# A hybrid decoder trunk on one core: modulation sums by transposes and in float32r, a 128-row gate product, and state products next to their value sums

## The chip, the cores and the metric

The kernel runs on one core of a Trainium2 chip. The metric is the device time of one execution in microseconds (us), as the median of several runs. A profile of one further execution shows each instruction of the engines: TensorE (PE, its weight loads as PEld), VectorE (DVE), ScalarE (ACT), GpSimd (POOL), and SyncE (SP), which issues most of the DMAs.

## What is computed

Two layers, each on x of 1024 tokens by 1024 columns, all in float32. In each, a conditioned norm, one wide projection to three groups of heads, and an output projection:

```python
c_act = silu(c)                                  # one row of 1024
mod = c_act @ w_mod + b_mod                      # 3072 columns
shift, scale, gate = split(mod, 3)
h = rms_norm(x, pre_gain) * (1 + scale) + shift
proj = h @ w_in                                  # 3088 columns
# A: sliding-window softmax attention; B: retention; C: gated linear attention
gate_logits = ga @ gla_gate_w + gla_gate_b       # rank 16, 128 columns
log_a = log_sigmoid(gate_logits) / 16
# C, per chunk: out = intra(scores, v) + (q * exp(b)) @ state
#               state = exp(b_last) * state + (k * exp(b_last - b)).T @ v
y = concat(a_out, r_out, g_out) @ w_out
x = x + gate * rms_norm(y, post_gain)
```

The change touches three pieces: the row `mod`, the `gate_logits`, and the state of C.

## The kernel before

Tokens are worked in 8 tiles of 128, in pairs p = 0 to 3. The large projections (`accum`, L521) are products of 128x128 weights with up to 512 columns, three passes over 8 blocks each: both factors are kept as a rounded float32r half and a float32r remainder in the tile `arena`, and the product of the two remainders is left out. Their sums go to PSUM tiles `mm` (3 banks); everything else goes to `aux` (5 banks). All matmuls are recorded by the helper `mult` (L171) and all transposes by `transp` (L186), so the profile names them by tiles. A product of plain float32 operands appears in the profile as two records for one instruction of the program, a float32r product and a transpose as one.

Working tiles come from shared pools: `t1` (256 columns, 7 buffers) and `t2` (512 columns, 14 buffers), both shown as `t`; `st` is a stage for weights, `sm` holds small columns.

The order on TensorE is fixed by a planner written in the kernel. It keeps a clock `clk`, to which `mult` and `transp` add an estimate per instruction. Jobs are generators: `yield lat("gc3", l)` means "come back when the clock has gone on by the time listed under that key", and `yield (t, flag)` waits for a flag as well. Between the products of a projection `pump` (L216) runs the jobs that are due. So another estimate, or a step on the other side of a `yield`, moves what follows by a few products. The orders of the other engines are laid out by the framework's scheduler from the same program.

- `mod_third(l, j)` (L356) makes one third of `mod` for a layer, in two halves `hh` of 512 columns. DVE accumulates 8 weight blocks, scaled by `c_act`, into `acc` of 128x512 (L384). The sum over the 128 partitions remains. For shift and scale (j < 2) it is wanted as a column: four products with `acc` as weights and one column of ones, then `mod_cols` (L288) adds the bias. For the gate (j = 2) it is wanted in every partition: ones (128x128) times `acc`, fp32, out 128x512, then a multiplication into `modg` (L398). Layer 0's shift and scale are made elsewhere (`mod_first`); `mod_third` runs with j = 2 in both layers, and with j = 1 and 0 for layer 1 while layer 0 is at work. Hence four column sums of four products each, and four gate sums.
- `gla_log` (L1068) multiplies `gwt` (17 of 32 rows used: 16 weights and the bias) with `gat`, the transposed low-rank columns and a row of ones; 32 rows by 512 columns, fp32, twice per layer. `new_ga` (L800) takes `gat` as a slice of a 128-partition buffer and fills it with ones on POOL.
- `gla_core` (L1136) is one pair of tiles of C. After `gc2`: a transpose of the keys to `kbn`, block products for the two tiles (out `bx`, `bd`), masking into `sc`; then the state products into `pst` (L1182: for each tile and head, 32 rows by 64 columns of output, fp32); then the delays `gc3` and `gc4`; then the value sums `within` (L1008: out 64x128, fp32, `aux<-sc,t`), for the first tile the product with the old state (`aux<-t,stG`), the update of `stC` from `pst` (L1202) and its spread to `stG` (L1203), both on DVE, a delay `gc6`, and the second tile's product with `stG`. The second update is the last reader of the decay factors `gs`, whose two buffers are cleared on POOL (L1117). The last pair has state products for its first tile only.

Of the kernel before, what the change touches and what calls it, by code (L numbers as in the profile page):

```python
# [10 lines left out]
F32 = mybir.dt.float32  # L11
# [6 lines left out]
P = 128  # L18
# [71 lines left out]
def trunk(ctx: ExitStack, tc: tile.TileContext, ins, cst, out):  # L90
# [79 lines left out]
    def mult(dst, lhsT, rhs, start, stop, cost=None):  # L170
        T.matmul(dst, lhsT, rhs, start=start, stop=stop)  # L171
        if cost is not None:
            clk[0] += cost
            return
        n = 1
        for d in rhs.shape[1:]:
            n *= d
        c = n / 2400.0
        if rhs.dtype == F32R:
            c = max(c, 0.107 if lhsT.shape[-1] > 64 else 0.055)  # L180
        else:
            c = max(4 * c, 0.21 if n > 2 else 0.03)
        clk[0] += c
# [5 lines left out]
    def lat(key, l):  # L189

        return L[key + "@1"] if l and key + "@1" in L else L[key]
# [96 lines left out]
    def mod_cols(l, j, hh, pm, rc):  # L288
        res = modc[(l, j)]
        ks = slice(4 * hh, 4 * hh + 4)  # L290
        if j == 0:
            V.tensor_tensor(res[:, ks], pm[:, 0:4], rc[:, ks], ALU.add)
        else:
            col = small(4)
            V.tensor_tensor(col, pm[:, 0:4], rc[:, ks], ALU.add)
            V.scalar_tensor_tensor(res[:, ks], col, 1.0, rc[:, 8 + 4 * hh:12 + 4 * hh], ALU.add, ALU.mult)
# [59 lines left out]
    def mod_third(l, j):  # L356
        wv = w_mod[l].rearrange("(p k) n -> p k n", k=KT)
        if j < 2:
            mod_tile(l, j)
            rows = mod_rows(l, j)  # L360
            yield lat("mod1", l)
            rc = mod_rows_t(rows)
        else:
            res = cp.tile([P, D], F32, name=nm("modg"), tag="modg")
            modg[l] = res
        for hh in range(2):
            c0 = j * D + 512 * hh
            acc = gp.tile([P, 512], F32, tag="acc", name=nm("acc"), bufs=1)
            if j == 2:
                G.memset(acc, 0.0)  # L370
                nc.sync.dma_start(acc[0:1, :], b_mod[l:l + 1, c0:c0 + 512])
            def fetch(k):
                w_ = stage()
                dma("lwm", w_, wv[:, k, c0:c0 + 512])
                return w_

            coming = fetch(0)
            for k in range(KT):
                wt, coming = coming, fetch(k + 1) if k + 1 < KT else None
                yield lat("mod7", l)  # L380
                if k == 0 and j < 2:
                    V.tensor_scalar(acc, wt, c_act[:, k:k + 1], None, ALU.mult)
                else:
                    V.scalar_tensor_tensor(acc, wt, c_act[:, k:k + 1], acc, ALU.mult, ALU.add)  # L384
                yield lat("mod2", l)
            yield lat("mod3", l)
            pm = aux()
            if j < 2:
                for b in range(4):
                    mult(pm[:, b:b + 1], acc[:, b * P:(b + 1) * P], ones[:, 0:1], True, True)  # L390
                mod_cols(l, j, hh, pm, rc)
                if j == 0:
                    flag(("modh", l, hh), lat("mod4", l))
            else:
                mult(pm, ones, acc, True, True)
                gain = stage()
                nc.sync.dma_start(gain, post_g[l:l + 1, 512 * hh:512 * hh + 512].to_broadcast((P, 512)))
                V.tensor_tensor(res[:, 512 * hh:512 * hh + 512], pm, gain, ALU.mult)  # L398
            yield lat("mod5", l)
        flag(("mod", l, j), lat("mod6", l))  # L400
# [397 lines left out]
    gat = []  # L798

    def new_ga():  # L800
        gat.append(gp.tile([P, NT * P], F32, tag="kT1", name=nm("gaT"), bufs=1)[0:32, 0:512])
        G.memset(gat[-1], 1.0)
    stR = cp.tile([P, 2, P], F32, name="stR")
    stG = cp.tile([P, 4, 64], F32, name="stG")
# [25 lines left out]
    for l in range(DEPTH):  # L830
        V.tensor_copy(sink8[:, l].rearrange("p (m r) -> p m r", r=2),
                      sinkn[:, 8 * l:8 * l + 8].rearrange("p (r m) -> p m r", r=2))
    gwt = cp.tile([32, 2, P], F32, name="gwt")
    V.memset(gwt, 0.0)
    for l in range(DEPTH):
        nc.sync.dma_start(gwt[0:16, l, :], gw_in[l])
# [299 lines left out]
    def gla_core(l, p, qk, vs):  # L1136
# [31 lines left out]
        for c in range(2):  # L1168
            if c:
                yield lat("gc7", l)  # L1170
            bx, bd = h4(aux()), h4(aux())
            for s in range(1, 4):
                q = slice(32 * s, 32 * s + 32)
                mult(bx[:, :, q], kxz[:, s - 1, c], qx[:, :, c, q], True, True)
            for s in range(4):
                i = slice(8 * s, 8 * s + 8)
                mult(blocks(bd)[:, :, :, i], kds[s][:, P * c:P * c + P], blocks(qd[:, :, c])[:, :, :, i], True, True)
            A.activation(scz[c][:, :, 32:P], bx[:, :, 32:P], AF.Copy)
            V.copy_predicated(scz[c], mask2.unsqueeze(1).to_broadcast((P, 4, P)), bd)
        pst = aux()  # L1180
        for c in range(2):
            if 2 * p + c < NT - 1:  # L1182
                for h in range(4):
                    mult(pst[32 * h:32 * h + 32, 64 * c:64 * c + 64], kbn[:, c * P + 32 * h:c * P + 32 * h + 32],
                         vs[c][:, 64 * h:64 * h + 64], True, True, 0.03)
        yield lat("gc3", l)
        yield lat("gc4", l)
        po = aux()
        for c in range(2):
            within(po, c, vs[c], scz[c])  # L1190
# [449 lines left out]
```

## Time and profile before

| | us |
|---|---|
| median of 3 runs | 957.99 (956.76 to 958.2) |
| the profiled execution | 954.65 |
| its span, first to last instruction | 952.9 |
| mean granted TensorE clock | 0.997 |
| TensorE busy | 932.7 |
| VectorE busy | 637.4 |
| ScalarE busy | 474.1 |
| GpSimd busy | 222.6 |

Busy times count an engine that executes an instruction; TensorE's records overlap, since products are pipelined, and their union is taken. A row of the timeline has start, length, engine, line, operation, tiles (out<-in), shape and count of merged instructions, and in brackets the idle time of the engine before it with what ended it. A row of a group has the busy time, the mean in ns, and the idle time before.

### The profile page before, as it was taken

The page shows a single profiled execution, that of the slowest core. Times are in us where ns is not written, and L with a number is a line of the kernel's source. Part 1 is how long each engine was busy: PE and PEld are TensorE (multiplying, and loading weights), DVE is VectorE, ACT ScalarE, POOL GpSimd, SP SyncE. Part 2 cuts the span into 40 slices and gives each one's busy share as a digit, 9 for nine tenths or more (in the row PEclk, how much of TensorE's full clock was granted, in tenths as well). Part 3 has the DMA queues.
Part 4 walks back from the last instruction along what each step waited for, and adds up shares of the span by engine and source line. Part 5 has one row for each costly group of instructions (what it writes and reads, how often), then busy time and mean ns, then how long its engine had stood idle before and what let it go on. Part 6 is the DMA issues. An engine that isn't in the chain of part 4 may idle for free.

```text
span 952.9 us, 15951 instructions
## 1 busy us (share of the span) xinstructions
PE 932.7 (98%) x5645; PEld 770.1 (81%) x5645; DVE 637.4 (67%) x1372; ACT 474.1 (50%) x1157; POOL 222.6 (23%) x288
## 2 busy tenths in 40 slices
PE   5999999999999999999999999999999999999997
PEld 1799887888888787778889888888888887787886
DVE  6886857757786988654685584694677787862332
ACT  3786233554756666622455532443667576661111
POOL 3222000423231324510131110033133033540000
PEclk9999999999999999999999999999999999999999
DMA  9943523613362345787455261362133222555951
GB/s 320 323 135 122 161 84 122 196 49 115 107 200 80 100 133 189 226 253 256 171 169 175 92 187 32 101 187 67 56 101 111 94 82 81 166 177 177 308 200 66
DMA packets 124651, 142.26 MB, mean 149 GB/s; under 512 B 11566, under 2 KB 95384, under 8 KB 124572
## 3 DMA queue, kind: packets, MB, share of 16 engines
q1 hardware_dynamic: 114396, 127.43, 42.1%
q10 hardware_dynamic: 10176, 13.82, 4.2%
q8 instruction: 44, 0.72, 0.3%
q14 instruction: 35, 0.29, 0.1%
HBM read 104.51 MB, written 36.70 MB: 148 GB/s over the span
## 4 chain that ended last, share of the span: by engine, by line
PE 85%; DVE 3%; issue 2%; ACT 2%; POOL 0%; DMA 0%; DVEq 0%; SPq 0%; POOLq 0%; ACTq 0%
PE mm L171 67%; PE aux L171 14%; PE aux L186 4%; ACT smx L971 0%; DMA t<-tabS 0%; ACT L1026 0%; DVE t L856 0%; ACT L1025 0%; DVE t L1029 0%; DVE t L1027 0%; DVE t L157 0%; ACT mx L1160 0%; DVE smx L966 0%; DVE arena L508 0%; DVE arena L149 0%
## 5 line engine op out<-in xcount | busy, mean ns | idle before, releaser
L171 PE MATMUL mm<-arena,arena 128*128 128x512 f32 (+2 forms) x1512 | 309.6, 358 | 0.0
L171 PE MATMUL mm<-arena 128*128 128x512 f32 (+2 forms) x1392 | 285.8, 359 | 0.0
L171 PEld LDWEIGHTS mm<-arena,arena 128*128 128x128 f32 x1512 | 246.5, 189 | 40.1 <-issue 2.1
L171 PEld LDWEIGHTS mm<-arena 128*128 128x128 f32 x1392 | 228.9, 190 | 37.2 <-issue 1.2
L171 PE MATMUL mm<-arena,mx 128*128 128x512 f32 (+1 forms) x696 | 157.3, 384 | 0.0
L171 PEld LDWEIGHTS mm<-arena,mx 128*128 128x128 f32 x696 | 126.5, 188 | 26.1 <-issue 1.5
L508 POOL TENSOR_TENSOR arena<-st,arena 128x512 fp32r<-128x512 f32 x57 | 85.9, 1512 | 158.0 <-ACT arena L147 100.3
L147 ACT ACTIVATE t<-aux 128x512 f32<-128x512 f32 x64 | 37.1, 591 | 82.6 <-PE aux L186 39.6
L508 DVE TENSOR_TENSOR arena<-st,arena 128x512 fp32r<-128x512 f32 x63 | 63.0, 1014 | 6.9 <-ACT arena L147 3.5
L147 ACT ACTIVATE arena<-st 128x512 fp32r<-128x512 f32 x82 | 48.4, 623 | 31.1 <-PE mm L171 15.0
L1285 ACT ACTIVATE t<-mm 128x512 f32<-128x512 f32 x30 | 17.9, 598 | 91.0 <-PE mm L171 46.3
L971 ACT ACTIVATE smx<-smx,sm 128x129 f32<-128x129 f32 x128 | 50.1, 394 | 18.1 <-DVE sm L968 17.9
L975 POOL TENSOR_TENSOR smx<-smx,sm 128x512 f32<-128x512 f32 x32 | 35.2, 1099 | 82.5 <-DVE sm L974 78.7
L384 DVE SCALAR_TENSOR_TENSOR acc<-st,c_act,acc 128x512 f32<-128x512 f32 x60 | 45.6, 760 | 13.1 <-DMA st<-in_w_mod_dram 12.1
L562 POOL TENSOR_TENSOR sm<-sm,few 128x1 f32<-128x1 f32 x26 | 14.8, 570 | 150.3 <-DVE sm L561 147.6
L1286 DVE TENSOR_TENSOR t<-mm,modg 128x512 f32<-128x512 f32 x30 | 20.7, 689 | 42.4 <-ACT t L1285 42.4
L1330 DVE SCALAR_TENSOR_TENSOR t<-t,sm,t 128x512 f32<-128x512 f32 x32 | 25.5, 827 | 30.8 <-DMA t<-xs 15.7
L186 PE MATMUL aux<-c_ident,t 128*128 128x128 f32 x224 | 33.7, 274 | 4.1 <-DVE t L634 2.3
L186 PEld LDWEIGHTS aux<-c_ident,t 128*128 128x128 f32 x224 | 26.6, 140 | 10.5 <-DVE t L634 2.7
L966 DVE COPY_PREDICATED smx<-c_curmask,aux 128x256 f32<-128x256 int32 x64 | 25.5, 447 | 12.8 <-ACT smx L147 11.4
L370 POOL MEMSET acc<- 128x512 f32 x4 | 2.1, 529 | 130.2 <-PE aux L171 119.1
L851 DVE TENSOR_TENSOR t<-mm,sincos 128x128 f32<-128x128 f32 (+2 forms) x36 | 16.2, 450 | 23.7 <-ACT t L147 12.5
(223 smaller groups left out, 1340.5 us busy)
## 6 DMA issues: line engine op xcount, KB each, us to landing
st<-in_w_in_dram SPq DMA_DIRECT2D x96, 256.0 KB, 3.9
st<-in_w_mod_dram SPq DMA_DIRECT2D x64, 256.0 KB, 3.0
mixS<-t SPq DMA_DIRECT2D x64, 256.0 KB, 2.5
mx<-mixS SPq DMA_DIRECT2D x28, 512.0 KB, 5.2
st<-in_w_out_dram SPq DMA_DIRECT2D x32, 256.0 KB, 3.2
wm<-in_w_mod_dram SPq DMA_DIRECT2D x12, 512.0 KB, 4.7
t<-in_x_dram SPq DMA_DIRECT2D x24, 256.0 KB, 4.9
t<-tabS SPq DMA_DIRECT2D x16, 256.0 KB
```

The lines of the kernel that those rows point to most:

```text
L147: A.activation(dst, src, AF.Copy)
L171: T.matmul(dst, lhsT, rhs, start=start, stop=stop)
L186: T.transpose(dst, src, idn)
L384: V.scalar_tensor_tensor(acc, wt, c_act[:, k:k + 1], acc, ALU.mult, ALU.add)
L508: i = (G if first == 0 and kc in LOG else V if first == 0 else eng(f"wlo{kc}")).tensor_tensor(wt[:, 1, 2 * kc:2 * kc + 2, 0:256], st, f(hi ...
L851: V.tensor_tensor(a4, s4, cs.unsqueeze(1).unsqueeze(1).to_broadcast((P, nh, 2, 32)), ALU.mult)
L966: V.copy_predicated(sv, curmask.unsqueeze(1).to_broadcast((P, 2, P)), pv[:, :, n // P - 1, :])
L971: A.activation(sm[:, h, :], sm[:, h, :], AF.Exp, bias=mx[:, h:h + 1], accum_out=sums[:, h:h + 1])
L975: eng("pn").tensor_tensor(sm[:, :, 0:128], sm[:, :, 0:128], rs.unsqueeze(2).to_broadcast((P, 4, P)), ALU.mult)
L1285: A.activation(yg, pm, AF.Square, accum_out=ss[:, nh:nh + 1])
L1286: V.tensor_tensor(yg, pm, modg[l][:, 512 * nh:512 * nh + 512], ALU.mult)
L1330: V.scalar_tensor_tensor(xt[j], yg[j], r, xt[j], ALU.mult, ALU.add)
```

## The change

1. Column sums (j < 2): `acc` is transposed in four blocks of 128 columns into one PSUM bank, and DVE adds each block along its columns (a reduction of 128x512 to 128x4).
2. Gate sums (j = 2): ScalarE copies the ones and a rounded `acc` (`hi`) to float32r, DVE makes the remainder `lo`, and two float32r products replace the fp32 product. The three new tiles come from `t1` and `t2`.
3. `gwt` and `gat` get 128 rows instead of 32; rows from 17 on of `gwt` are zero.
4. In `gla_core` the two delays come ahead of the state products, so that these stand directly ahead of `within`, and their PSUM bank is taken there.

```diff
@@ mod_third
+            if j == 2:
+                one, hi, lo = t1(F32R), t2(F32R), t2(F32R)
+                A.activation(one[:, 0:P], ones, AF.Copy)
+                A.activation(hi, acc, AF.Copy)
+                V.tensor_tensor(lo, acc, f(hi), ALU.subtract)
             yield lat("mod3", l)
             pm = aux()
             if j < 2:
                 for b in range(4):
-                    mult(pm[:, b:b + 1], acc[:, b * P:(b + 1) * P], ones[:, 0:1], True, True)
-                mod_cols(l, j, hh, pm, rc)
+                    transp(pm[:, b * P:(b + 1) * P], acc[:, b * P:(b + 1) * P], ident)
+                sums = small(4)
+                V.tensor_reduce(sums, pm.rearrange("p (b n) -> p b n", b=4), AX.X, ALU.add)
+                mod_cols(l, j, hh, sums, rc)
                 if j == 0:
                     flag(("modh", l, hh), lat("mod4", l))
             else:
-                mult(pm, ones, acc, True, True)
+                mult(pm, one[:, 0:P], hi, True, False)
+                mult(pm, one[:, 0:P], lo, False, True)
@@ new_ga
-        gat.append(gp.tile([P, NT * P], F32, tag="kT1", name=nm("gaT"), bufs=1)[0:32, 0:512])
+        gat.append(gp.tile([P, NT * P], F32, tag="kT1", name=nm("gaT"), bufs=1)[:, 0:512])
@@ trunk
-    gwt = cp.tile([32, 2, P], F32, name="gwt")
+    gwt = cp.tile([P, 2, P], F32, name="gwt")
@@ gla_core
+        yield lat("gc3", l)
+        yield lat("gc4", l)
         pst = aux()
         for c in range(2):
             if 2 * p + c < NT - 1:
                 for h in range(4):
                     mult(pst[32 * h:32 * h + 32, 64 * c:64 * c + 64], kbn[:, c * P + 32 * h:c * P + 32 * h + 32],
                          vs[c][:, 64 * h:64 * h + 64], True, True, 0.03)
-        yield lat("gc3", l)
-        yield lat("gc4", l)
         po = aux()
```

What this does to the orders is shown at three places. First TensorE in layer 1, first pair, before (each row is an instruction of the program with its count; `mm_7201` is a projection, `aux_7231` the block products, `aux_7241` the state products, `aux_7258` the value sums):

```order
L171 MATMUL aux_7231<-mx_6900,t_1247_7129 128x16x8
L171 MATMUL aux_7241<-t_1228_7041,t_1263_7213 32x64 x4
L171 MATMUL aux_7241<-t_1239_7092,t_1263_7213 32x64 x4
L171 MATMUL mm_7201<-arena_357 128x512 x8
L171 MATMUL aux_7258<-sc_6905,t_1228_7041 64x128 x4
L171 MATMUL aux_7258<-sc_6906,t_1239_7092 64x128 x4
```

And now, with the same parts as `aux_7267`, `aux_7285` and `aux_7294`:

```order
L171 MATMUL aux_7267<-mx_6918,t_1263_7164 128x16x8
L171 MATMUL mm_7237<-arena_357 128x512 x8
L171 MATMUL aux_7285<-t_1244_7076,t_1279_7249 32x64 x4
L171 MATMUL aux_7285<-t_1255_7127,t_1279_7249 32x64 x4
L171 MATMUL aux_7294<-sc_6923,t_1244_7076 64x128 x4
L171 MATMUL aux_7294<-sc_6924,t_1255_7127 64x128 x4
```

The state products went behind the eight projection products and touch the value sums; so they do in all eight pairs. Second, VectorE in layer 0, second pair, before: the masking of the scores (`sc`), then the first state update, and only later its spread:

```order
L1179 COPY_PREDICATED sc_2057<-c_mask_418,aux_2637 128x4x128
L1202 SCALAR_TENSOR_TENSOR stC<-stC,gs_2319,aux_2647 128x64
L1145 TENSOR_TENSOR t_469_2773<-t_394_2362,t_429_2534 128x512
L1032 TENSOR_TENSOR t_436_2562<-t_433_2558,t_435_2561 128x512
L868 TENSOR_TENSOR kT_2168<-aux_2658,kT_2167 128x128
```

And now, at the place of the update (rows L859 to L865 are a rotation of keys):

```order
L876 TENSOR_TENSOR kT_2181<-aux_2707,kT_2180 128x128
L864 TENSOR_TENSOR t_460_2692<-t_461_2693,t_462_2694 128x2x32
L865 TENSOR_TENSOR t_460_2692<-t_461_2693,t_462_2694 128x2x32
L1210 SCALAR_TENSOR_TENSOR stC<-stC,gs_2333,aux_2716 128x64
L1211 TENSOR_TENSOR stG<-stC,c_hmask 128x256
```

The update stands some fifteen rows further back in the queue, directly ahead of its spread. Third, VectorE where the attention scores begin, now: mask copies into `smx`, the new reduction of a column sum (`sm_3710`), the first step of the next accumulator, and the softmax maximum (`sm_3717`):

```order
L974 COPY_PREDICATED smx_3669<-c_curmask,aux_3674 128x2x128
L947 COPY smx_4011<-sink_434 128x4
L947 COPY smx_4029<-sink_434 128x4
L397 TENSOR_REDUCE sm_3710<-aux_3705 128x4
L382 TENSOR_SCALAR acc_3817<-st_3818,c_act 128x512
L295 TENSOR_TENSOR sm_3712<-sm_3710,sm_2391 128x4
L976 TENSOR_REDUCE sm_3717<-smx_3652 128x4
```

Before, the maximum followed its two mask copies at once:

```order
L966 COPY_PREDICATED smx_3636<-c_curmask,aux_3639 128x2x128
L966 COPY_PREDICATED smx_3636<-c_curmask,aux_3640 128x2x128
L968 TENSOR_REDUCE sm_3691<-smx_3636 128x4
L966 COPY_PREDICATED smx_3653<-c_curmask,aux_3657 128x2x128
L939 COPY smx_3994<-sink_434 128x4
```

The column sum came later there, behind the rotations of the queries.

## The prediction

> **What bounds the kernel now.** I read the page's busy times first, then the waits of TensorE, then the chain that ended last, and only then single places of TensorE's timeline. The page:
>
> ```profile
> PE 932.7 (98%) x5645; PEld 770.1 (81%) x5645; DVE 637.4 (67%) x1372; ACT 474.1 (50%) x1157; POOL 222.6 (23%) x288
> PEclk9999999999999999999999999999999999999999
> PE 85%; DVE 3%; issue 2%; ACT 2%; POOL 0%; DMA 0%; DVEq 0%; SPq 0%; POOLq 0%; ACTq 0%
> ```
>
> TensorE is busy in 98% of the span at full clock, and 85% of the chain is its own work. A busy TensorE could still be one that waits inside its queue, so the waits come next (engine and line, what it waited for, us in total, times, longest):
>
> ```profile
> PE aux L186 <- DVE posr L425: 6.1, 1, 6.1
> PE aux L186 <- DVE t L634: 2.3, 1, 2.3
> PE aux L186 <- DVE smx L966: 1.7, 3, 0.9
> ```
>
> These are the three longest. The rows of 6.1 and 2.3 us belong to the start; within the two layers nothing is above 1.7 us, in three pieces. So no other engine sets the pace, and a microsecond of TensorE's issue time removed is a microsecond of the span, unless the new order makes it wait. The unit for this issue time is a projection product, which I take from the longest unbroken piece of the chain:
>
> ```profile
> 871.27 70.05 PE mm L171 x308
> ```
>
> 70.05 / 308 = 0.2274 us each. The durations in the groups are of no use for a sum, because products overlap; I count from start to start and take off 0.2274 us per projection product in between.
>
> **Column sums of the modulation (four times, all in layer 0, for layer 1).** Before: four products of one column, eight records in fp32. After: four transposes.
>
> ```profile
> 462.06 0.60 PE L186 MATMUL aux<-c_ident,t 128*128 128x128 f32 x4
> 462.42 3.00 PE L171 MATMUL mm<-arena,mx 128*128 128x512 f32 x12
> 465.26 0.94 PE L171 MATMUL aux<-c_ones,acc 128*128 128x1 f32 x8
> 466.06 1.19 PE L171 MATMUL mm<-arena,mx 128*128 128x512 f32 x4
> 467.09 1.47 PE L186 MATMUL aux<-c_ident,t 128*128 128x128 f32 x12
> ```
>
> The sums: 467.09 - 465.26 = 1.83, less 4 x 0.2274 = 0.91, gives 0.92 us. Four transposes: 465.26 - 462.06 = 3.20, less 12 x 0.2274 = 2.73, gives 0.47 us. Saved: 0.45 us, four times 1.8 us. The replacement is seen in this very stage, so I give this term no wide bounds.
>
> A rule speaks against this term. The Trainium skill, page "TensorE: Matmul & The Clock Gate", section "Part 4: PE-mode transpose", gives about 275 ns for a transpose in a kernel and says that the full clock does not engage for it; section "Back-to-back issue gap" gives some 60 cycles for a product of up to 64 columns. An estimate by these two: 4 x 0.275 = 1.1 us against 8 x 0.025 = 0.2 us, so 0.9 us lost each time, 3.6 us in all, and a sum of 1.0 us instead of 6.4, 957.0 us. The trace has the transposes at a pitch that fits neither: four cost 0.47 us with the clock at 9 throughout, and the eight records cost 0.92, each with a weight load of its own (the page counts 5645 loads to 5645 products). I take the rows.
>
> **Gate sums (four times, two per layer).** Before: ones times the accumulated 128x512 in fp32. After: the accumulator in a rounded half and a remainder, two products in float32r. The same pair, with the same shape, stands in every head norm (out aux, in t and bones).
>
> ```profile
> 150.20 1.02 PE L171 MATMUL aux<-acc,c_ones 128*128 128x512 f32 x2
> 150.66 2.42 PE L171 MATMUL mm<-arena,arena 128*128 128x512 f32 x8
> 152.92 0.60 PE L186 MATMUL aux<-c_ident,t 128*128 128x128 f32 x4
> 664.45 0.62 PE L171 MATMUL aux<-t,bones 128*128 128x512 f32 x2
> 664.91 2.00 PE L171 MATMUL mm<-arena 128*128 128x512 f32 x8
> 666.75 1.02 PE L171 MATMUL aux<-acc,c_ones 128*128 128x512 f32 x2
> ```
>
> fp32: 152.92 - 150.20 = 2.72, less 8 x 0.2274 = 1.82, gives 0.90 us. The pair: 2.30 - 1.82 = 0.48 us. Saved: 0.42 us, four times 1.7 us.
>
> **Low-rank product (four times).** It stays fp32 with 512 columns; its contraction grows from 32 to 128 rows, of which 111 meet zero weights.
>
> ```profile
> 107.73 2.67 PE L171 MATMUL mm<-arena,arena 128*128 128x512 f32 x11
> 110.34 1.12 PE L171 MATMUL aux<-gaT,gwt 32*128 32x512 f32 x2
> 111.39 1.20 PE L171 MATMUL mm<-arena,arena 128*128 128x512 f32 x4
> 112.42 0.60 PE L186 MATMUL aux<-c_ident,t 128*128 128x128 f32 x4
> ```
>
> 112.42 - 110.34 = 2.08, less 0.91, gives 1.17 us; the eleven products ahead take 2.61 instead of 2.50, so entering it costs another 0.11. Together 1.28 us, against 0.90 us for the gate sum, the same product with 128 rows. Saved: 0.38 us, four times 1.5 us. The lower bound is nothing, if the operand and not the row count makes it slow; I take 1.5, the nearest row being one of the same type and columns. The memsets of both operands cover more partitions with the same columns: on POOL and DVE at the start, nothing for TensorE.
>
> Here, too, a rule differs: in the same page's section "Why this matters for your kernels" a small product with 32 rows takes as long as one with 128. By it this term is 0 and the sum 4.9 us. The rows show 1.28 against 0.90; no row here has both depths of one operand.
>
> **State products (eight times).** The 8 or 16 records (out 32 x 64) move from behind the block products to just ahead of the value sums (out 64 x 128). Both use part of the array's columns, so one switch between whole and part should vanish.
>
> ```profile
> 671.62 1.50 PE L171 MATMUL aux<-mx,mx 128*128 128x128 f32 x12
> 673.10 1.17 PE L171 MATMUL mm<-arena 128*128 128x512 f32 x4
> 674.11 1.50 PE L171 MATMUL aux<-mx,mx 128*128 128x128 f32 x12
> 675.76 0.43 PE L171 MATMUL aux<-t,t 128*32 128x64 f32 x16
> 676.12 2.11 PE L171 MATMUL mm<-arena 128*128 128x512 f32 x8
> 678.16 1.10 PE L171 MATMUL aux<-sc,t 128*64 128x128 f32 x16
> ```
>
> Without them: 674.11 - 671.62 = 2.49, less 0.91, is 1.58 us for the block products. With them: 678.16 - 674.11 = 4.05, less 8 x 0.2274 = 1.82, is 2.23; the difference of 0.65 holds an entry of some 0.11 into the value sums, so they cost 0.54 us, of which 0.36 (675.76 to 676.12) is their own stretch. Beside the value sums no row shows them. Bounds: a switch of 0.11 more than now (eight times, 0.9 us lost), or a complete overlap (0.54 x 8 = 4.3 us gained). I take their own stretch, 0.18 us saved, eight times 1.4 us.
>
> The step issues no DMA. It is moved past projection products on TensorE; on DVE the update of stC, which reads it, is moved with it, and on POOL the memset of gs, which waits for stC's second update in layer 0's first pair: now at 223.40, then some 3.3 us later. The next POOL row starts at 227.37, so that queue loses nothing:
>
> ```profile
> 223.40 0.14 POOL L1117 MEMSET gs<- 128x50 f32 x1 [3.67 <-DVE stC L1202]
> 227.37 0.46 POOL L944 TENSOR_TENSOR vd<-va,va 128x128 f32<-128x128 f32 x1 [3.83 <-ACT va L881]
> ```
>
> **What is added beside TensorE.** Four reductions of 128x512 on DVE, four subtractions there, four rounding copies and four small copies on ScalarE:
>
> ```profile
> L968 DVE TENSOR_REDUCE sm<-smx 128x4 f32<-128x516 f32 x32 | 21.7, 677 | 0.5
> L1020 DVE TENSOR_TENSOR t<-t,t 128x512 fp32r<-128x512 f32 x16 | 11.0, 688 | 13.3 <-ACT t L147 10.1 <-issue 3.1
> L147 ACT ACTIVATE t<-t 128x512 fp32r<-128x512 f32 x32 | 20.2, 630 | 15.5 <-DVE t L1029 14.4 <-DMA sgS<-t 0.6
> 87.25 0.31 ACT L1408 ACTIVATE bones<-t 128x128 fp32r<-128x128 f32 x1
> 105.57 0.75 DVE L384 SCALAR_TENSOR_TENSOR acc<-st,c_act,acc 128x512 f32<-128x512 f32 x1
> ```
>
> That is 4 x 0.677 + 4 x 0.688 = 5.5 us on DVE and 4 x 0.630 + 4 x 0.31 = 3.8 us on ScalarE. Cover: the first accumulator is complete at 106.32 (last row) and its product starts at 150.20, so the halves have 44 us. The rounding copy waits on ScalarE for that accumulate, and behind it stand a head norm's table load and exponential; DVE's subtraction waits for the copy; neither queue is one that TensorE waits for by more than the rows above. On SP the modulation's weight fetches change places with others by a few rows, under the same cover. The reductions sit in DVE's queue behind the transposes; the worst place is the start of the attention scores, where one now stands ahead of the first softmax maximum and holds it up by about 2.5 us (itself, the new accumulator's first step of 0.48 and two mask copies). Without cover, DVE's 5.5 us would be the price.
>
> **Sum.** 1.8 + 1.7 + 1.5 + 1.4 = 6.4 us; with all bounds 2.6 to 9.3. The profiled execution took 954.65 us, so 948.3 us; it lies 3.3 us under the median of the runs, 957.99, and the same difference there gives 951.6 us.
>
> **Rivals.** First, a part fails: the low-rank product stays as slow with 128 rows, or the state products save nothing, or both, so 3.5 to 5 us, 953 to 954.5 us. For it speaks that neither is seen in its new form. Second, the gain is eaten: if DVE's 5.5 us show, 0.9 us are left, 957.1 us; against it speak the 44 us of cover. Within this case stands dear transposes, if they cost more than the 0.47 us of the row; the rows are of the same operation in the same stage, so it has 0.01 of the chance (the Trainium skill's rule on transposes, above, would come to this). Third, more than the sum: the state products overlap the value sums completely, 4.3 us instead of 1.4, so 948.7 us; against it, that they now take 0.36 us of their own where nothing hinders them. Fourth, slower: the state chain becomes late. In layer 1 the second half's products follow the value sums closely, and stG must be ready:
>
> ```profile
> 239.95 0.43 PE L171 MATMUL aux<-t,t 128*32 128x64 f32 x16
> 244.30 0.27 DVE L1202 SCALAR_TENSOR_TENSOR stC<-stC,gs,aux 128x64 f32<-128x64 f32 x1
> 725.85 1.09 PE L171 MATMUL aux<-sc,t 128*64 128x128 f32 x16
> 727.76 0.41 DVE L1203 TENSOR_TENSOR stG<-stC,c_hmask 128x256 f32<-128x256 f32 x1
> 728.81 0.61 PE L171 MATMUL aux<-t,stG 128*128 128x128 f32 x4
> ```
>
> From the state products' new place to those products are 2.96 + 0.36 = 3.3 us; stC and stG need 0.7. In layer 0 DVE came 4.35 us after the products to the update. Were it as late in layer 1's four pairs, each would wait 1.7 us, 6.8 in all, and the gain were gone; from there each further 0.5 us of lateness costs 2 us, so at 5 us the time is 961 us. Against it: stG waits for the first half's products in any case, and DVE's order has the update directly ahead of stG.
>
> **Chances.** The sum as worked out (949 to 953 us): 0.60; a part fails: 0.17; more: 0.06; eaten: 0.10; slower: 0.07. This measurement tells about 0.2%, 1.9 us, from no change. Faster by more: 0.60 + 0.17 + 0.06 = 0.83; same 0.10; slower 0.07. The range from 947.5 to 956 us leaves out the last two cases; its low end lets the third case take the 1.7 us of TensorE's wait for L966 with it, less a little.
>
> **What would show it.** In the changed profile four transposes with acc in place of 128x1 products; pairs of t,t at 128x512 costing 0.48 us; gaT,gwt with 128 rows costing 0.90; value sums starting some 0.36 us after the state products; TensorE's waits still below 2 us each. A wait of TensorE on DVE stG, or on DVE smx longer than now, would make the prediction wrong.

## The result: 0.6% slower, and the profile after

| | before | after |
|---|---|---|
| median of 8 runs, us | 958.15 (956.66 to 960.79) | 964.45 (962.12 to 965.17) |
| the profiled execution, us | 954.65 | 962.81 |
| its span, us | 952.9 | 961.1 |

The ratio is 1.0059, 95% interval 1.0044 to 1.0073; 951.6 us were forecast, in a range of 947.5 to 956. Of the eight runs of the changed kernel the three with a mean granted clock of 0.994 to 0.996 took 962.1 to 962.8 us, the profiled one among them, and the five with 0.990 to 0.992 took 964.4 to 965.2. The page of the changed kernel, busy times and chain:

```profile
PE 931.3 (97%) x5629; PEld 768.7 (80%) x5629; DVE 646.0 (67%) x1380; ACT 478.0 (50%) x1165; POOL 225.5 (23%) x288
PE 83%; DVE 5%; DMA 4%; issue 3%; ACT 3%; POOL 1%; SPq 0%; ACTq 0%; DVEq 0%; POOLq 0%
```

TensorE has less work, but less of the chain is its own. The two longest of its waits within the layers after the change (us in total, times, longest):

```profile
PE aux L186 <- DVE t L1226: 3.9, 3, 3.3
PE aux L171 <- ACT t L147: 3.4, 1, 3.4
```

Before the change the longest waits of these two kinds were 0.5 and 0.6 us. The four replaced operations in TensorE's timeline after the change, each with the rows that it is counted from:

```profile
111.50 1.02 PE L171 MATMUL aux<-gaT,gwt 128*128 128x512 f32 x2
111.95 1.50 PE L171 MATMUL mm<-arena,arena 128*128 128x512 f32 x4
113.29 0.60 PE L186 MATMUL aux<-c_ident,t 128*128 128x128 f32 x4
...
155.63 0.62 PE L171 MATMUL aux<-t,t 128*128 128x512 f32 x2
156.09 1.98 PE L171 MATMUL mm<-arena,arena 128*128 128x512 f32 x8
157.91 0.60 PE L186 MATMUL aux<-c_ident,t 128*128 128x128 f32 x4
...
462.94 0.60 PE L186 MATMUL aux<-c_ident,acc 128*128 128x128 f32 x4
463.29 1.17 PE L171 MATMUL mm<-arena,mx 128*128 128x512 f32 x4
464.30 1.03 PE L186 MATMUL aux<-c_ident,t 128*128 128x128 f32 x8
...
678.72 1.85 PE L171 MATMUL aux<-mx,mx 128*128 128x128 f32 x12
...
681.55 1.50 PE L171 MATMUL aux<-mx,mx 128*128 128x128 f32 x12
...
685.05 0.43 PE L171 MATMUL aux<-t,t 128*32 128x64 f32 x16
685.41 1.09 PE L171 MATMUL aux<-sc,t 128*64 128x128 f32 x16
686.43 2.13 PE L171 MATMUL mm<-arena 128*128 128x512 f32 x8
688.40 0.61 PE L171 MATMUL aux<-t,stG 128*128 128x128 f32 x4
```

From start to start, less 0.2274 us per projection product: low-rank 1.79 - 0.91 = 0.88 us, the pair 2.28 - 1.82 = 0.46, a column sum 1.36 - 0.91 = 0.45; the last four rows and the block ahead 6.85 - 16 x 0.2274 = 3.21 us, against 3.40 before (674.11 to 681.15). At these places the forecast savings come, each to 0.02 us. Counted in the same way at all their places they are some 6 us in all, against the 6.4 of the sum; the low-rank products are the smaller ones, 0.27 to 0.38 us each.

The first new wait, in TensorE's timeline of before and of after, with ScalarE's copy that releases it (the turned queries of the retention, `ret_turn`), and the clock (stretch, then busy times; the third number from the end is the granted clock):

```profile
135.04 0.71 PE L171 MATMUL aux<-t 64*128 64x128 f32 x8 [0.58 <-ACT t L147]
```
```profile
138.88 0.71 PE L171 MATMUL aux<-t 64*128 64x128 f32 x8 [3.42 <-ACT t L147]
139.53 3.13 PE L171 MATMUL mm<-arena 128*128 128x512 f32 x8
138.23 0.60 ACT L147 ACTIVATE t<-aux 128x512 f32<-128x512 f32 x1 [0.81 <-DMA mixS<-t]
```
```profile
140.00:144.00 4.00, 4.00 (x20) 3.02 (x20) 3.87 (x8) 0.45 (x1) 0.00 (x0) 0.57 0.43 116
```

The copy waits for a DMA: its t2 buffer is still being stored by a head norm. And the wait costs more than itself, since the clock then falls to about half: eight projection products take 2.93 us instead of 1.82 (139.53 to the next row, 142.46). The second, in layer 1; DVE's rows are a rotation (L859 to L865) with the head norm (L1035, L1037) in its midst:

```profile
604.29 0.68 DVE L859 TENSOR_TENSOR t<-mm,sincos 128x512 f32<-128x512 f32 x1
608.35 0.69 DVE L1035 TENSOR_TENSOR t<-t,t 128x512 f32<-128x512 f32 x1 [2.42 <-ACT t L1034]
609.07 0.69 DVE L1037 TENSOR_TENSOR t<-aux,t 128x512 f32<-128x512 f32 x1
609.79 0.42 DVE L861 TENSOR_TENSOR t<-mm,sincos 128x256 f32<-128x256 f32 x1
612.82 0.63 PE L186 MATMUL aux<-c_ident,t 128*128 128x128 f32 x4 [3.34 <-DVE t L1226]
```

The rotation's second product (L861) comes 5.5 us after the first. In the built program its buffer is the one that the head norm's scale holds until L1037; before the change the head norm came after the whole rotation.

### The profile page after: what moved, and what is told of

The parts are those of the page before. It is cut to its first block, busy times and chain, and to the rows that moved or that the text cites. A ratio compares the mean times of both kernels' runs of the same rounds, so it can differ in the third digit from the quotient of the medians.

```text
span 961.1 us, 15937 instructions
## 1 busy us (share of the span) xinstructions
PE 931.3 (97%) x5629; PEld 768.7 (80%) x5629; DVE 646.0 (67%) x1380; ACT 478.0 (50%) x1165; POOL 225.5 (23%) x288
## 4 chain that ended last, share of the span: by engine, by line
PE 83%; DVE 5%; DMA 4%; issue 3%; ACT 3%; POOL 1%; SPq 0%; ACTq 0%; DVEq 0%; POOLq 0%
PE mm L171 66%; PE aux L171 13%; PE aux L186 4%; DVE arena L516 1%; DMA xk<-in_x_dram 1%; DMA t<-aoS 1%; DMA aoS<-t 1%; DMA c_freq<-cst_freq_dram 0%; ACT smx L979 0%; DMA st<-in_w_in_dram 0%; ACT L1033 0%; DMA st<-in_w_out_dram 0%; POOL arena L516 0%; DMA t<-tabS 0%; ACT t L1033 0%
## 5 line engine op out<-in xcount | busy, mean ns | idle before, releaser
L384 DVE SCALAR_TENSOR_TENSOR acc<-st,c_act,acc 128x512 f32<-128x512 f32 x60 | 47.4, 790 | 15.7 <-DMA st<-in_w_mod_dram 13.0
L662 ACT ACTIVATE t<-aux,mod,mod 128x128 f32<-128x128 f32 x56 | 21.3, 454 | 17.8 <-PE aux L186 10.7
L1035 DVE TENSOR_TENSOR t<-t,t 128x512 f32<-128x512 f32 x16 | 11.1, 691 | 28.2 <-ACT t L1034 25.0
```

Source lines behind the costliest of these rows:

```text
L662: A.activation(hf[:, ks], pt[:, ks], AF.Identity, scale=gain, bias=shift)
```

## The experiments

Each was run beside the kernel before on the same chip; ratios are to it, with the 95% interval. The last two columns are worked out from TensorE's timeline, as differences to the profile of before: the idle time after 50 us in which TensorE waited (3.7 us before), and what is left of the time from the 140th to the last projection product without it (896.3 before). The time up to the 140th is left out: it took 46.8 us in the profile of before and 48.3 to 51.0 in all others, also in one with the orders of before, so 2 us of the difference between the two profiles is not the change. Both columns come from one execution each. Their sum is up to 3.4 us more than the difference of the medians (for e6, profiled at 961.68 us, and e9, at 962.36), so they say where the time goes, and the ratio says what a version is worth. "Waits" counts from the end of the last instruction; in full flow the next one would have begun before that end (a transpose lasts 0.27 us, and the next follows after 0.11), so each wait also puts some 0.16 us into "the rest".

| kernel | median | ratio | waits | the rest |
|---|---|---|---|---|
| changed | 964.45 | 1.0059 (1.0044 to 1.0073) | +8.2 | -2.0 |
| e1_no_gate | 956.63 | 0.9985 (0.9975 to 0.9996) | +3.5 | -2.7 |
| e2_gate_only | 967.44 | 1.0097 (1.0082 to 1.0111) | +8.6 | +2.8 |
| e3_late | 956.04 | 0.9971 (0.9962 to 0.9980) | +2.0 | -4.5 |
| e4_clock | 963.92 | 1.0053 (1.0034 to 1.0073) | +7.5 | -0.7 |
| e5_rings | 962.03 | 1.0037 (1.0025 to 1.0049) | +5.8 | -0.8 |
| e6_rings_clock | 959.97 | 1.0020 (1.0012 to 1.0029) | +6.2 | -0.9 |
| e7_state_only | 958.87 | 1.0013 (1.0004 to 1.0021) | +2.7 | -0.6 |
| e8_gate_rank | 962.47 | 1.0049 (1.0035 to 1.0063) | +6.4 | -0.1 |
| e9_hold_acc | 959.29 | 1.0012 (1.0001 to 1.0023) | +4.0 | +0.5 |
| e10_state_gs3 | 963.11 | 1.0045 (1.0032 to 1.0058) | +1.2 | +5.9 |
| e11_all | 961.73 | 1.0047 (1.0028 to 1.0066) | +4.3 | +3.0 |
| e12_three | 958.15 | 0.9993 (0.9982 to 1.0004) | +2.7 | -3.0 |
| e13_gs3_aligned | 956.67 | 0.9986 (0.9976 to 0.9995) | +1.5 | -0.9 |
| e14_late_gs3 | 955.68 | 0.9979 (0.9970 to 0.9988) | +4.1 | -3.2 |
| e15_shift32 | 964.09 | 1.0071 (1.0057 to 1.0086) | -0.4 | +6.8 |
| e16_late_three | 958.01 | 1.0002 (0.9993 to 1.0011) | +4.8 | -2.4 |
| e17_late_hold | 957.12 | 0.9988 (0.9979 to 0.9997) | +4.6 | -4.2 |
| e18_late_hold_gs3 | 957.08 | 0.9989 (0.9978 to 1.0000) | +4.8 | -4.5 |

### Which part, and is it the buffers, the order or the added work?

e1_no_gate takes the gate sums back:

```diff
-                one, hi, lo = t1(F32R), t2(F32R), t2(F32R)
-                ...
-                mult(pm, one[:, 0:P], hi, True, False)
-                mult(pm, one[:, 0:P], lo, False, True)
+                mult(pm, ones, acc, True, True)
```

> The changed kernel with the gate sums left as they were, one fp32 product each: no halves, no copy of the ones; column sums, 128-row low-rank product and moved state products stay. Theory 'buffers' (the two halves hold two of the 14 t2 buffers and one t1 buffer for some 20 us, and rotation, turn of the queries and head norm wait for a buffer): no wait of TensorE of 3 us at 135 or 609 us; 958.15 - 1.8 - 1.5 - 1.4 = 953.5 us, 952 to 955.5. Rival 'order' (the planner's clock runs differently, so products are issued before their operands are ready): the column sums and the moved state products still shift the order, about half of the loss stays, 957 to 961 us. Rival 'queues' (the added copies and subtractions themselves stand ahead of urgent work on ScalarE and VectorE): as for buffers, but the reductions stay, 953.5 to 955.

Both long waits are gone; the loss came with the gate sums. But 0.15% are gained, not 0.5%: a wait of 1.7 us at 241 us and one of 1.1 at 744 stand in their place.

e2_gate_only does the gate sums alone, e4_clock the whole change, both with the planner's old costs (in e4 also 0.03 us for each transpose of a column sum):

```diff
-                mult(pm, one[:, 0:P], hi, True, False)
-                mult(pm, one[:, 0:P], lo, False, True)
+                mult(pm, one[:, 0:P], hi, True, False, 0.427)
+                mult(pm, one[:, 0:P], lo, False, True, 0.427)
```

> The kernel before with the gate sums alone changed, and the planner told the old cost of 0.853 us for the pair, so that TensorE's order is the old one word for word but for the pair. Buffers: two to four long waits near 135 and 605 us come back, 958.15 - 1.7 + 6 to 9 = 962 to 965.5 us. Order: no new wait, 956.5 us. Queues: each of four places loses 1.6 us (two copies and a subtraction) at most, 956.5 to 961 us.

> The whole change, with the planner told the old costs (0.853 us for the pair, 0.03 us for each transpose of a column sum), so that TensorE's order around 135 and 609 us is that of before. Buffers: the waits stay, 961 to 965 us. Order: they go, 952 to 954 us. Queues: 958 to 963 us.

Both waits are there in both, to 0.1 us (3.44 and 3.35, 3.40 and 3.31), with TensorE's old order at those places. So the shift of the order is not the cause. e2 lies above its range, at 967.44 us: it lacks what the other three parts save, and in its profile the clock fell behind both waits. Here is the second, which in the changed kernel's profile went by at full clock (1.00 from 612 to 616 us):

```profile
616.69 1.09 PE L186 MATMUL aux<-c_ident,t 128*128 128x128 f32 x4 [3.35 <-DVE t L1224]
617.43 2.06 PE L171 MATMUL mm<-arena 128*128 128x512 f32 x4
```
```profile
616.00:620.00 4.00, 3.31 (x10) 2.83 (x11) 2.47 (x6) 0.60 (x1) 0.00 (x0) 0.57 0.20 68
```

e3_late keeps the arithmetic and makes the halves 4 us ahead of their product:

```diff
+            yield lat("mod3", l) - (4.0 if j == 2 else 0.0)
             if j == 2:
                 one, hi, lo = t1(F32R), t2(F32R), t2(F32R)
                 ...
-            yield lat("mod3", l)
+                yield 4.0
```

> The changed kernel with the halves made 4 us of planner time ahead of their products instead of 15 to 17.6 us; TensorE's order stays that of the changed kernel but for one pair, which moves by one projection. The added work is the same. Buffers: the hold falls from some 20 to some 5 us, the waits at 135 and 609 us go, 952 to 955 us. Order: nothing changes, 964 us. Queues: the added work only moves, 960 to 965 us. If the pair now waits for its own halves, each such wait would show on TensorE as a wait for L389 or L390.

The same two places in e3_late: the first wait is back at its old 0.59 us, the second gone, and no half clock behind them.

```profile
136.39 0.71 PE L171 MATMUL aux<-t 64*128 64x128 f32 x8 [0.59 <-ACT t L147]
...
604.74 0.60 PE L186 MATMUL aux<-c_ident,t 128*128 128x128 f32 x4
```

8.4 us against the changed kernel come from moving three instructions of each half, and no version has a lower ratio; at 956.04 us it is still above the 952 to 955 of its expectation. The move shortens the hold, but it also moves the added work; e5 tells these apart.

### The same place, other buffers

e5_rings leaves the halves where the change makes them, in buffers of rings idle there; e6_rings_clock adds the old costs.

```diff
-                one, hi, lo = t1(F32R), t2(F32R), t2(F32R)
+                one = gp.tile([P, P], F32R, tag="vd", name=nm("one"), bufs=VDF)
+                hi, lo = [gp.tile([P, 4, 129], F32R, tag="smx", name=nm("half"), bufs=SMB)
+                          .rearrange("p a b -> p (a b)")[:, 0:512] for _ in range(2)]
```

> The changed kernel with the two halves in buffers of the softmax ring (tag smx, idle in these stages) and the ones in the ring vd; the halves are made at the same place of the program and held as long, and TensorE's order is that of the changed kernel, word for word. Buffers: the waits of 3.4 and 3.3 us at 139 and 613 us go without any copy being moved, 953 to 957 us (the late halves gave 956.0 against 959.0 for the kernel before). Queues (the copies and subtractions themselves delay others): the waits stay, 960 to 964 us.

> As e5_rings, and the planner told the old costs of the pair and of the column sums' transposes, as in e4_clock, so that the order of before is left only where the state products move it. If what e3_late lost against the sum (3.5 us) comes from the order, 952.5 to 955 us; if not, as e5_rings, 953 to 957 us.

e8_gate_rank is the kernel before with these gate sums, the old costs and the 128-row product:

> The kernel before with the gate sums as float32r pairs from the idle rings and the low-rank product 128 rows deep, the planner told the old cost, so that TensorE's order is that of before. By the terms of the sum: 958.96 - 1.7 - 1.5 = 955.8 us, no new wait. If 128 rows save nothing, 957.3 us. If the copies delay others, 958 us or more.

The waits at 139 and 613 us are gone in all three, so the t2 buffers did make them. The first place in e5:

```profile
138.53 0.71 PE L171 MATMUL aux<-t 64*128 64x128 f32 x8 [0.58 <-ACT t L147]
```

But a new one of 3.1 to 3.3 us stands at 196 to 198 us in each, in e5 and e6 with the half clock behind it, and all three missed the time of the theory that they were built on: buffers were not the whole cause. In e8, DVE, POOL and TensorE there:

```profile
190.93 3.19 DVE L382 TENSOR_SCALAR acc<-st,c_act 128x512 f32<-128x512 f32 x1 [0.28 <-DMA st<-in_w_mod_dram]
194.15 1.54 DVE L384 SCALAR_TENSOR_TENSOR acc<-st,c_act,acc 128x512 f32<-128x512 f32 x2
195.60 1.41 DVE L1256 TENSOR_TENSOR t<-aux,c_causal 128x256 f32<-128x256 f32 x4
190.04 3.79 POOL L823 MEMSET mx<- 128x512 f32 x8
196.07 1.65 PE L171 MATMUL aux<-t,t 128*64 128x128 f32 x16 [3.13 <-DVE t L1256]
```

The fp32 product read `acc` until it was done; the remainder sets `acc`, a single buffer, free at once. So the next accumulator's first steps (L382, L384) come at 191 us instead of 213, ahead of the masks (L1256) that TensorE waits for. e9_hold_acc adds to e8 a late reader of `acc`:

```diff
                 V.tensor_tensor(res[:, 512 * hh:512 * hh + 512], pm, gain, ALU.mult)
+                V.tensor_tensor(small(1), pm[:, 0:1], acc[:, 0:1], ALU.add)
```

> As e8_gate_rank, and after each gate product VectorE reads one column of the old accumulator (a 128x1 addition), so that the accumulator's single buffer is given back behind the product, as before the change, and not as soon as the remainder is made. Theory 'early release': e8's wait of 3.13 us at 196 us comes from the next accumulator's first three steps, which the release lets in ahead of the masks of the retention scores (the first of them took 3.19 instead of 0.48 us beside GpSimd's memset); it goes, with the half-clock microseconds behind it, 954.5 to 956.5 us (958.1 - 3.2 plus the four additions). Rival: the rounding copies on ScalarE or the remainder on VectorE delay the masks themselves; the wait at 196 us stays, 960 us or more.

The wait at 196 us goes, as early release says; but one of 1.68 us at 192.7 comes, behind the rounding copy on ScalarE (L391), which the turn's copy has to let pass:

```profile
191.52 0.63 ACT L391 ACTIVATE half<-acc 128x512 fp32r<-128x512 f32 x1 [0.25 <-DVE acc L384]
192.06 0.58 ACT L147 ACTIVATE t<-aux 128x512 f32<-128x512 f32 x1
192.69 0.72 PE L171 MATMUL aux<-t 64*128 64x128 f32 x8 [1.68 <-ACT t L147]
```

So at this one place a part of the rival is right, too: a rounding copy does delay urgent work, though not the masks. The time is 0.12% above that of before, and the 954.5 to 956.5 us of the expectation are missed.

### The moved state products alone

e7_state_only moves the delays and nothing else; e10_state_gs3 gives it a third buffer for `gs`.

```diff
-        g = gp.tile([P, 2, 25], F32, tag="gs", name=nm("gs"), bufs=2)
+        g = gp.tile([P, 2, 25], F32, tag="gs", name=nm("gs"), bufs=3)
```

> The kernel before with the two delays ahead of the state products, nothing else. The term of the sum: 958.96 - 1.4 = 957.6 us, no new wait. Rival: the new place is what causes the waits of 1.1 to 1.7 us that all of e1_no_gate, e3_late and the changed kernel show between 219 and 245 us or at 745 us (head norm, keys of the state), 958.5 to 960.5 us.

> As e7_state_only, with three buffers instead of two for the decay factors gs. Theory 'gs': the second update of stC, late by 8.4 us in e7, holds back the memset of the next gs, its exponential on ScalarE, and behind that the head norm's square, so TensorE waits 1.84 us at 240 us; with a third buffer the wait goes, and 958.87 falls by some 1.5 us to 956.5 to 958 us. Rival: the head norm is late for another reason, 958.5 to 959.5 us. The wait of 1.13 us at 744 us is not touched by either.

By itself this part costs 0.13%, as its rival had it. In e7 the memset of `gs` comes at 231.80 us, not 3.3 but 8.4 us later than the 223.40 of before; POOL, ScalarE and TensorE of e7:

```profile
231.80 0.14 POOL L1117 MEMSET gs<- 128x50 f32 x1 [3.48 <-DVE stC L1202]
232.66 0.24 ACT L1124 ACTIVATE gs<-gs 128x50 f32<-128x50 f32 x1 [4.88 <-DVE gs L1121]
234.49 0.59 ACT L1018 ACTIVATE t<-aux 128x512 f32<-128x512 f32 x1
239.65 0.50 PE L171 MATMUL aux<-t,bones 128*128 128x512 f32 x1 [1.84 <-DVE t L1020]
```

The exponential of `gs` (L1124) stands in ScalarE's queue ahead of the head norm's square (L1018), which came at 231.67 before. With a third buffer this wait is gone, but e10 is slower by 0.45%, in "the rest": 224 bytes more moved the operand tile `arena1` from byte 163584 to 163808, and products that read it ran slower. e13_gs3_aligned takes the bytes out of a pad ahead and keeps the address, e15_shift32 is the kernel before with 224 unused bytes:

```diff
+        if not dec:
+            gp.tile([P, 56], F32, tag="pad2", name="padg", bufs=1)
```

> As e10_state_gs3, but the third gs buffer (224 bytes per partition) is made good by a smaller pad ahead and 32 bytes behind, so that the projections' operand tile (arena1) and everything after gs keep the addresses of before; what lies between the pad and gs moves by 256 bytes. In e10 the projections from arena1 ran at 234 and 232 ns instead of 227, and the wait of 1.84 us at 240 us was gone. Theory 'address' for that pitch together with 'gs' for the wait: pitch 227 ns, no wait at 240 us, 956.5 to 958 us. If the pitch has another cause than the address, 962 to 964 us as e10.

> The kernel before with an unused tile of 224 bytes per partition behind gs, so that arena1 begins at byte 163808 instead of 163584 (a multiple of 32, no longer of 64); the orders of all engines are those of before, row for row. Theory 'address': pitch of the products from arena1 234 and 232 instead of 227 ns, some 1500 products by 5 to 7 ns less what other shapes gain, 4 to 6 us more: 963 to 965 us. Rival, that e10's pitch came from the order or from something else on the chip: 958 to 960 us.

Both times are as the theory says. The long stretch of the chain in e15, against 70.05 us for the same 308 products in before:

```profile
877.48 72.07 PE mm L171 x308
```

That is 0.2340 us each instead of 0.2274, with the orders of before. But not every product from `arena1` is slower. A row of 44 whose operands both lie in `arena1`, before and in e15:

```profile
317.57 10.13 PE L171 MATMUL mm<-arena 128*128 128x512 f32 x44
```
```profile
320.24 10.14 PE L171 MATMUL mm<-arena 128*128 128x512 f32 x44
```

And the products of 512 columns that pair the two arenas, as a group, before and in e15; the number behind the bar is the busy time in us:

```profile
L171 PE MATMUL mm<-arena,arena 128*128 128x512 f32 x984 | 241.5, 397 | 0.0
```
```profile
L171 PE MATMUL mm<-arena,arena 128*128 128x512 f32 x984 | 245.6, 401 | 0.0
```

The loss of 6.8 us sits in products that pair `arena1` with a tile that did not move: 4.1 us with the other arena, and 2.8 us in the 648 products of an arena and `mx` (151.3 to 154.1 us). The 912 with both operands in one arena went from 223.1 to 223.5 us. So what counts here is how the two operands lie to each other. A shift by 224 bytes does it; in e13 `mx` lies 256 bytes lower than before, and the same 648 products take 151.0 us. No other shift was tried. In e13 the wait at 240 us is gone and 0.14% are gained, as the term of 1.4 us would have it.

### All together

e11_all joins the four parts, the idle rings, the held accumulator and three `gs` buffers; e12_three is the same without the state products and with two `gs` buffers; e14_late_gs3 is e3_late with the aligned third buffer; e16_late_three has the column sums, the low-rank product and late halves, with the old costs; e17_late_hold and e18_late_hold_gs3 are e3_late and e14_late_gs3 with the held accumulator.

> All four parts of the change, with halves in the idle rings, the accumulator held until its product, three buffers for gs and the old costs for the planner. If the three causes (t2 buffers, early release, gs) are all, the sum of 6.4 us comes but for the wait of 1.1 us at 745 us: 952 to 954.5 us. If something further eats the gain, 955 us or more.

> As e11_all without the moved state products: column sums by transposes, gate sums as pairs, low-rank product with 128 rows, TensorE's order that of before word for word. By the sum 958.1 - 1.8 - 1.7 - 1.5 = 953.1 us, 952.5 to 954.5 us. If the reductions of the column sums show on VectorE, 954.5 to 956 us. Faster than e11_all if the moved state products lose more in waits than their 1.4 us.

> e3_late (the whole change with late halves, 956.0 us) with the third gs buffer of e13. If the moved state products still cost through gs there, 954 to 955.5 us; if not, as e3_late, 955.5 to 957 us.

> Three parts of the change (column sums, gate sums with late halves in t2 and t1, 128-row low-rank product), the state products left in place, and the planner told the old costs, so that TensorE's order is that of before but for one pair. By the terms 958.6 - 5.0 = 953.6 us if no wait appears; with the waits of 0.4 to 1.1 us of e12_three, 955 to 957 us. If it comes below e3_late (956.0 us), the moved state products lose more than they gain in the whole change, too.

> The whole change with late halves (e3_late) and the accumulator's buffer held until its product, by the 128x1 addition of e9. In e3_late and e16_late_three six steps of the next accumulator stand on VectorE ahead of the gate's decay sums at 211 to 216 us, and TensorE waits 1.15 and 1.3 us for a key copy at 219 us. Theory 'early release': that wait goes and 954.5 to 955.5 us come out (e3_late 956.0 against 959.0 for the kernel before, ratio 0.997; here 0.995 to 0.997). Rival: other waits take its place, ratio 0.998 or above.

> e17_late_hold with the third gs buffer of e13. If the gs buffers still cost beside the rest, 0.5 to 1.5 us less than e17_late_hold; if not, the same within 0.5 us.

e11 has the shifted `arena1` (72.07 us for the 308 products), so its time tells nothing. The others lie between 0.9979 and 1.0002: none comes to the sum. e12 and e16 missed their expectations, e17 came out as its rival; e14 and e18 say that the `gs` buffers no longer matter beside the rest. A part of what eats the gain is seen in e16, where five steps of the next accumulator from 209 us on, the last behind a DMA, stand ahead of the gate's decay sums; DVE, ScalarE, TensorE:

```profile
215.19 0.75 DVE L384 SCALAR_TENSOR_TENSOR acc<-st,c_act,acc 128x512 f32<-128x512 f32 x1 [0.70 <-DMA st<-in_w_mod_dram]
219.44 0.36 ACT L1176 ACTIVATE t<-aux 128x256 f32<-128x256 f32 x1
219.86 0.94 PE L171 MATMUL aux<-mx,mx 128*128 128x128 f32 x6 [1.30 <-ACT t L1176]
```

Before, that key copy ended at 214.11 us and nothing waited. In e17, with the accumulator held, this wait is gone, as expected; instead there is one of 1.40 us at 187 and one of 1.11 at 624. The wait of 1.1 us near 744 is in most versions, 0.24 in before and 0.25 in e3_late. In e12 a DVE operation of the same shape as POOL's takes 1.77 us, against 0.68 in before; e12 first:

```profile
728.51 1.77 DVE L519 TENSOR_TENSOR arena<-st,arena 128x512 fp32r<-128x512 f32 x1
728.33 1.40 POOL L519 TENSOR_TENSOR arena<-st,arena 128x512 fp32r<-128x512 f32 x1 [0.44 <-PE mm L171]
```
```profile
728.10 0.68 DVE L508 TENSOR_TENSOR arena<-st,arena 128x512 fp32r<-128x512 f32 x1
728.09 1.83 POOL L508 TENSOR_TENSOR arena<-st,arena 128x512 fp32r<-128x512 f32 x1 [0.60 <-PE mm L171]
```

Started within 0.01 us of each other DVE keeps its pace; 0.18 us behind POOL it loses 1.1 us, and the chain of the head norm and the key copy behind it is as much later. The profiles of the other versions say the same. In 17 of the 20 this DVE operation began 0.08 to 0.33 us behind POOL's, took 1.76 or 1.77 us, and the wait is 1.13 or 1.14. In the other three (before, e3_late, e15_shift32) it began at most 0.04 us behind, took 0.68 us, and the wait is 0.16 to 0.25. So some 0.9 us hang on a tenth of a microsecond that no part of the change aims at. No run moves this one start alone.

## Why the prediction was wrong

- **The four terms of the sum.** Right: 0.47, 0.44, 0.40 and 0.19 us saved a piece at the places shown, against 0.45, 0.42, 0.38 and 0.18, and some 6 us over all places. The Trainium skill's figure for a transpose, about 275 ns (page "TensorE: Matmul & The Clock Gate", section "Part 4: PE-mode transpose"), fits the length of one here, 0.27 us, but it is no price in full flow: four cost 0.45 us, at full clock. The rule of the Trainium skill on 32 rows (same page, section "Why this matters for your kernels") does not hold for this fp32 product: the same operand shows 1.28 us with 32 rows and 0.88 with 128.
- **The cover of the halves: the step that failed.** The 44 us between the complete accumulator and its product were taken as cover for the work. They were also the time for which two of 14 t2 buffers (and one of 7 t1) would be held, and that had no term. It cost two waits of 3.4 and 3.3 us, and half clock. e2, e3 and e5 show it.
- **"Neither queue is one that TensorE waits for by more than the rows above".** Wrong as a ground: waits of under 0.6 us meant that those queues were just in time, not that they had room. e9 shows 1.68 us behind one rounding copy of 0.63.
- **The release of `acc`.** Not seen at all: the fp32 product kept the next accumulation back. Freed earlier, it took DVE ahead of the masks (3.13 us in e8) or of the decay sums (1.30 us in e16).
- **The reductions on VectorE.** The place that was feared did not show: at the start of the attention scores TensorE waits 0.92 and 0.58 us for `smx`, as before (0.93 and 0.58). That the total for `smx` rose from 1.7 to 2.6 us comes from later places (0.81 us at 394), where no reduction stands ahead.
- **The memset of `gs`.** Found, but its delay was put at 3.3 us (8.4 in e7), and only POOL's queue was asked, not ScalarE's exponential and the head norm behind it: 1.84 us in e7, and the part alone loses. The slower rival named the state chain, but for `stG`; no version waits for `stG` by more than 0.21 us.
- **"A microsecond of TensorE's issue removed is a microsecond of the span".** In the changed kernel the rest fell by 2.0 us only: some 6 saved, some 1.5 given back by the half clock at 140 us (139.53 to 145.50 took 5.97 us, the same products in e8 4.43), and 2.5 more. About 1 us of these is the lost overlap at the waits, of which there are 14 after 50 us instead of 9; the block products at 678.72, for one, took 1.85 us with a wait of 0.11 in their midst, the same ones at 681.55 took 1.50. The remainder is not itemised.

What stays open is why none of the repaired versions comes to the sum. The waits that each shows are named, and the one near 744 is traced to its start; that the order was fitted to the old durations everywhere is only an argument.

## What to carry to other kernels

Price a new working tile by how long it holds its buffer, not only by the work that fills it, and ask of each tile that is now read earlier or later what its release lets in, and ahead of whom. Where the bound engine shows many waits of half a microsecond, its producers are just in time: expect a part of what is taken off the bound engine to come back as such waits, as in the versions here. Make short-lived operands as late as their consumer allows. And when an experiment changes the number of buffers, keep the operand tiles at their old addresses, or at least at their old places to each other.

## What the hardware showed that was not expected

- Of nine waits of 3.1 to 3.4 us (two each in the changed kernel, e2 and e4, one each in e5, e6 and e8) seven were followed by half the granted clock, five for 3.4 us and two (the first of e4, and e6: 0.57 on average from 194 to 202 us) for 6.8; so was one of 1.68 us in e9, for 3.4. Waits of 1.84 us in e7 and 1.73 in e1 were not. The Trainium skill, page "TensorE: Matmul & The Clock Gate", section "Why this matters for your kernels", says that gaps over about 3 us do it; the trace agrees for seven of nine, while 3.34 us at full clock and 1.68 us at half show that the gap's length alone does not decide.
- How the addresses of a product's two operands lie to each other sets its pace. With `arena1` moved by 224 bytes, products of it and an unmoved tile took 0.2340 instead of 0.2274 us, those with both operands in it the same as before (44 in 10.14 us against 10.13); the kernel lost 0.71% (e15).
- A TENSOR_SCALAR on VectorE took 3.19 instead of 0.48 us beside GpSimd's memsets, and a TENSOR_TENSOR 1.77 instead of 0.68. The Trainium skill, page "GPSIMD Engine Reference", section "1. Specifications", says that the two share SBUF interfaces; the trace agrees. Which of the two starts first decides: over the 20 profiles, that TENSOR_TENSOR took at most 0.70 us in the 249 cases in which it began up to 0.6 us ahead of GpSimd's or at most 0.05 behind, and 1.42 to 1.78 us in the 174 in which it began 0.1 to 0.6 us behind.
